# RWKV layer of a hybrid trunk: r as three fp32r products, weights split one layer earlier, inputs and joins moved

## Chip, cores and metric

One core of a Trainium2 chip runs the whole program once. The metric is device time in microseconds. TensorE is called PE, its weight loads PEld, VectorE DVE, ScalarE ACT, GpSimd POOL and SyncE SP, as in the profile.

## What is computed

Two layers on 256 tokens of width 1024. Each layer is FFN, mixer, FFN and a gated per-layer embedding, with RMS norms around every part. The mixer of layer 0 is a gMLP, that of layer 1 an RWKV-7 time mixer. The change touches the RWKV mixer and the FFN in front of it:

```python
dx = shift(h) - h
x_rkv = h[:, :, None, :] + dx[:, :, None, :] * mu[:3]
r, k, v = einsum('bsnd,nde->bsne', x_rkv, w_in)          # three 1024 x 1024 products
zw = w0 + tanh((h + dx * mu[3]) @ w1) @ w2               # decay
a  = sigmoid(a0 + ((h + dx * mu[4]) @ a1) @ a2)
g  = sigmoid((h + dx * mu[5]) @ g1) @ g2                 # gate
kk = normalised(k * k_k); k = k * (1 + (a - 1) * k_a)
S_t = S_{t-1} diag(w_t) + (S_{t-1} a_t) b_t^T + v_t k_t^T;  y_t = S_t r_t
out = ((group_norm(y) + bonus) * g) @ w_out
swiglu(x) = (silu(gate) * up) @ w2,  gate, up = split(x @ w13)   # the FFN
```

All inputs are float32, D = 1024, 16 heads of 64, D_FF = 2816.

## The kernel before

**Weights.** `self.units` is the list of all weight pieces, in the order in which the program wants them. Most are 128 x 1024 pieces in three steps. `emit_dma` (L127) loads one into one of four `raw` buffers. `emit_split` (L137) takes one of 20 slots of 128 x 2048 and writes the fp32r high half (ACT, L154) and the remainder (DVE, L156) into it. A product is then three fp32r products: high by high, low by high, high by low (`mm3`, L178 to L180). A piece with a fourth entry is not split: it is loaded as it is, 1 MB at a time, into a slot (L146), and multiplied as float32, which the profile shows as two records for each product. `pump(k, reserve)` emits up to k pieces if slots are left, `need(i)` emits all pieces up to i at once, `release(i)` gives the slot back. Slots and the eight PSUM banks are handed out first in, first out, so each user waits for the last user of the same slot or bank.

**Order on the engines.** The program is written in one order; the framework places the instructions of each engine in a queue, where a later instruction can go ahead of an earlier one that is not ready, and adds the waits. `with behind(name)` keeps the instructions of its block behind a named one of the same engine.

**The FFN ahead of RWKV.** Eleven column blocks c. From c = 2 on, one iteration is `AT(c)` (L400, 64 products: 32 of 512 columns and 32 of 256) and the down products of block c - 2 (`Dn`, L178 to L180, 24 of 512 columns). Each iteration uses six pieces: four of w13 and two of w2.

**RWKV** (`rwkv`, one function with inner helpers), in program order:
- `K(0)`, `K(1)`: k, 16 steps of three fp32r products; then `l1()`, the first product of decay and a.
- `xprod(n)` (L819, DVE): the input h + dx mu of one of the six uses, eight pieces of 128 x 256. `xprod(0)` for r comes here; `xprod(5)` for the gate and `xprod(2)` for v come after the decay.
- `low(g)`: second product of decay and a, with ACT's tanh and sigmoid. `squares(i)` (ACT), `knorm(b)` (L895 to L904: DVE, ACT, POOL) and `ktr(b)` (PE transposes, L913).
- For each half i: `decay(i)` (L999 to L1004, DVE), `ab(i)` (L1010 to L1013), some of r's eight steps (`r_step`, L1055, float32, 256 columns) and `triangle(i)` (L1039, small products, copied out by ACT).
- The substitution (L1091, L1093, DVE, 15 steps that depend on each other), two transposes (L1094, L1095).
- rT copies (L1250), `xprod(5)`, `gate1` (L1171), `xprod(2)`, the products that form kT, sk and rT x gam (L1256 to L1269).
- v: eight steps of eight records (`v_step`, L1307, float32, 512 columns). Between them the gate's second product, and four `join`s, which put the 16 x 16 inverses together (small products: L1110, L1121, L1136, L1150). `join(0)` to `join(2)` stand among steps 5 to 7. `inside(k)` (L1284 to L1294) forms one of eight pairs of masked products: PE, DVE, PE. `inside(0)` to `(3)` stand among the v steps, `(4)` and `(5)` behind them.
- `tb` transposes, `join(3)`, `inside(6)`, `inside(7)`, then the mean of v and `stack_v` (L1389, DVE, eight pieces).
- Four `chunk`s, each depending on the one before: `us` (L1415, L1441), `y`, `st` (L1453), with L1443, L1444 and L1458 on ACT and DVE between. Between the chunks stand weight splits and `vgain` (L1244, L1245). Then the output product (`Dn`, `o`).

Of the kernel before, what the change touches and what calls it, by code (L numbers as in the profile page):

```python
# [60 lines left out]
class Trunk:  # L61
    NSLOT = 20

    def __init__(self, ctx, tc, io):
        self.tc = tc
        self.nc = tc.nc
        self.io = io
        self.uid = 0
        ep = lambda name, bufs=1, **k: ctx.enter_context(tc.tile_pool(name=name, bufs=bufs, **k))
        self.slots = ep("slots")  # L70
        self.pp = ep("pp", space=bass.MemoryType.PSUM)
        self.rawp = ep("raw", 4)
# [17 lines left out]
        self.pq = {}  # L90

# [35 lines left out]
    def emit_dma(self):  # L127
        i = self.n_dma
        self.n_dma += 1
        if len(self.units[i]) > 3:  # L130
            return
        src, p, n = self.units[i]
        t = self.rawp.tile([128, 1024], F32, name="raw", tag="raw")
        self.nc.sync.dma_start(t[:p, :n], src)
        self.raw[i] = t

    def emit_split(self):  # L137
# [3 lines left out]
        if len(self.units[i]) > 3:  # L141
# [8 lines left out]
        src, p, n = self.units[i]  # L150
# [155 lines left out]
    def ffn_units(self, f):  # L306
# [468 lines left out]
    def rwkv_units(self):  # L775
# [9 lines left out]
        put("r", rows(0))  # L785
# [6 lines left out]
    def rwkv(self, at):  # L792
# [20 lines left out]
        def xprod(n, lo=0, hi=T, ks=range(KT)):  # L813
# [135 lines left out]
        xprod(0)  # L949
        wu_ = self.slot("wu")  # L950
# [100 lines left out]
        def r_step(k):  # L1051

            w = self.need(at["r"] + k // 2)[0][:, k % 2]
            for m in range(KT):
                mm(psr[m // 2][:, (m % 2) * T:(m % 2 + 1) * T], lhsT=w[:, m * 128:(m + 1) * 128], rhs=xent(0, k),  # L1055
                   start=k == 0 and m % 2 == 0, stop=k == KT - 1 and m % 2 == 1)
            if k % 2:
                self.release(at["r"] + k // 2)
# [12 lines left out]
        self.drop(eo)  # L1071
        self.drop(X["x"][0])
# [22 lines left out]
        V.transpose(xt.rearrange("p n t -> p t n"), Wu)  # L1095
# [173 lines left out]
        V.tensor_tensor(kT, kT, rT, op=ALU.mult)  # L1269
        self.drop(gam, ta, rT)  # L1270
# [54 lines left out]
        v_step(3)  # L1325
        v_step(4)
# [13 lines left out]
        v_step(7, join(2))  # L1340
# [6 lines left out]
        inside(4)  # L1347
        inside(5)
# [27 lines left out]

        sv = [self.slot("sv") for _ in range(2)]
        svv = [t.rearrange("p (c m h t) -> p c m h t", c=2, m=8, h=2) for t in sv]
        vv = vn.rearrange("p (b m h t) -> p b m h t", b=2, m=8, h=2)
        vm = self.small(32, "vm", 1)  # L1380
        vmv = vm.rearrange("p (b m h) -> p b m h", b=2, h=2)
        for b in range(NB):
            V.tensor_reduce(vm[:, b * 16:(b + 1) * 16], vn[:, b * D:(b + 1) * D].rearrange("p (h t) -> p h t", t=64), axis=AX.X, op=ALU.add)
            V.tensor_scalar(vm[:, b * 16:(b + 1) * 16], vm[:, b * 16:(b + 1) * 16], ck[:, 0:1], 1.0 / 64, op0=ALU.mult, op1=ALU.mult)

        def stack_v(c):
            rs = half[c % 2]
            for h in range(2):
                V.scalar_tensor_tensor(svv[c // 2][half[1 - h], c % 2, :, h, :], vv[rs, c // 2, :, h, :], ck[rs, 0:1],  # L1389
                                       vmv[rs, c // 2, :, h].unsqueeze(2).to_broadcast([64, 8, 64]), op0=ALU.mult, op1=ALU.subtract)  # L1390

        for c in range(NCH):
            stack_v(c)
        G.memset(svv[0][EV, 0, :, 0, :], 0.0)
        G.memset(svv[0][OD, 0, :, 1, :], 0.0)
# [284 lines left out]
```

## Time and profile before

| | us |
|---|---|
| median of 3 runs | 1177.98 |
| lowest, highest | 1177.35, 1180.4 |
| the profiled execution | 1183.38 |
| its span, first to last instruction | 1181.6 |

The profile is that of one execution. Times in it are counted from the start of its span. The RWKV stage lies between about 745 us (first product of k) and 958 us, the FFN ahead of it between about 565 and 745. An engine's queue is in order: an instruction that waits holds up all behind it. The idle time ahead of an instruction is put down to what ended last by semaphore events.

### The profile page before, as it was taken

Reading aid. Unit: us, or ns where it says so; the run is one execution under the profiler, and the core shown is the slowest. Engines: PE = TensorE matmul, PEld = TensorE weight load, DVE = VectorE, ACT = ScalarE, POOL = GpSimd, SP = SyncE. Lnnn points to the kernel's source line nnn. Section 1 sums busy time; section 2 is a strip of 40 time slices with the busy share of each in tenths; the row PEclk is TensorE's granted clock in tenths of the full one; section 3 lists DMA queues with packets and bytes.
Section 4 is the critical chain, followed back from the end, with each engine's and each line's share of the span. In section 5 each row is a group of like instructions: output and inputs, shape, how many; then the busy total and the mean of one; then the engine's idle time right before and its main releaser. Section 6 shows DMA issues by size and latency. Waiting matters only on the chain. (4 is left out here: it accounts for less than half of the span.)

```text
span 1181.6 us, 18709 instructions
## 1 busy us (share of the span) xinstructions
PE 1151.2 (97%) x7284; PEld 954.3 (81%) x7284; DVE 859.1 (73%) x1299; ACT 659.7 (56%) x1145; POOL 72.5 (6%) x92
## 2 busy tenths in 40 slices
PE   8999999999999999999999999999998899999997
PEld 6788888888888888888888888777467778888886
DVE  5886666877678666667876666878859898676663
ACT  6665556545476555558755554374226396555553
POOL 0000000010010000001100000230000220000011
PEclk8999999999999999999999999999989999999999
DMA  7886654746586666646766664550300377666510
GB/s 244 292 295 196 190 172 152 253 156 205 186 271 202 194 192 184 192 134 196 248 189 194 193 192 144 178 183 1 125 4 21 108 249 263 193 189 193 177 47 36
DMA packets 58841, 207.78 MB, mean 176 GB/s; under 512 B 6784, under 2 KB 7296, under 8 KB 58496
## 3 DMA queue, kind: packets, MB, share of 16 engines
q1 hardware_dynamic: 58752, 206.59, 54.8%
q8 instruction: 57, 0.93, 0.3%
q14 instruction: 32, 0.26, 0.1%
HBM read 205.51 MB, written 1.05 MB: 175 GB/s over the span
## 5 line engine op out<-in xcount | busy, mean ns | idle before, releaser
L156 DVE TENSOR_TENSOR w<-raw,w 128x1024 fp32r<-128x1024 f32 x348 | 423.6, 1223 | 145.6 <-ACT w L154 139.8
L154 ACT CAST w<-raw 128x1024 fp32r<-128x1024 f32 x348 | 366.3, 1055 | 153.9 <-PE mm L400 68.7
L400 PE MATMUL mm<-xT,w 128*128 128x512 f32 (+1 forms) x2304 | 407.8, 337 | 0.0
L400 PEld LDWEIGHTS mm<-xT,w 128*128 128x128 f32 x2304 | 358.6, 189 | 50.0
L178 PE MATMUL acc<-w,hT 128*128 128x512 f32 x352 | 138.2, 393 | 0.0
L179 PE MATMUL acc<-w,hT 128*128 128x512 f32 x352 | 137.3, 390 | 0.0
L180 PE MATMUL acc<-w,hT 128*128 128x512 f32 x352 | 137.1, 389 | 0.0
L408 ACT COPY pn<-mm 128x256 f32<-128x256 f32 x144 | 46.6, 375 | 93.8 <-PE mm L400 93.8
L409 DVE TENSOR_TENSOR pn<-mm,pn 128x256 f32<-128x256 f32 x144 | 54.4, 418 | 39.3 <-ACT pn L408 39.3
L180 PEld LDWEIGHTS acc<-w,hT 128*128 128x128 f32 x352 | 66.1, 188 | 14.1
L178 PEld LDWEIGHTS acc<-w,hT 128*128 128x128 f32 x352 | 66.2, 188 | 12.6
L179 PEld LDWEIGHTS acc<-w,hT 128*128 128x128 f32 x352 | 66.3, 188 | 12.3
L232 POOL TENSOR_SCALAR rpost<-ss 128x1 f32<-128x1 f32 x15 | 7.5, 500 | 777.9 <-ACT junk L239 777.9
L178 PE MATMUL mm<-w,xT 128*128 128x512 f32 x128 | 51.8, 415 | 2.9 <-ACT w L154 2.6
L289 DVE SCALAR_TENSOR_TENSOR xT<-tr,gT,xT 128x128 fp32r<-128x128 f32 x112 | 35.6, 344 | 24.4 <-ACT xT L288 23.5
L179 PE MATMUL mm<-w,xT 128*128 128x512 f32 x128 | 51.4, 405 | 0.7 <-DVE xT L289 0.5
L412 DVE TENSOR_TENSOR pn<-pn,yc 128x512 f32<-128x512 f32 x72 | 49.7, 691 | 2.0
L180 PE MATMUL mm<-w,xT 128*128 128x512 f32 x128 | 50.9, 403 | 0.0
L179 PE MATMUL z<-w,xT 128*128 128x512 f32 x128 | 49.9, 390 | 0.0
L180 PE MATMUL z<-w,xT 128*128 128x512 f32 x128 | 49.9, 390 | 0.0
L178 PE MATMUL z<-w,xT 128*128 128x512 f32 x128 | 49.7, 393 | 0.0
L288 ACT ACTIVATE xT<-tr,gT 128x128 fp32r<-128x128 f32 x112 | 37.8, 371 | 19.3 <-PE tr L275 14.9
(282 smaller groups left out, 1534.8 us busy)
## 6 DMA issues: line engine op xcount, KB each, us to landing
raw<-in_w SPq DMA_DIRECT2D x264, 512.0 KB, 4.3
raw<-in_win SPq DMA_DIRECT2D x32, 512.0 KB, 4.4
raw<-in_wout SPq DMA_DIRECT2D x16, 512.0 KB, 4.8
raw<-in_wg SPq DMA_DIRECT2D x16, 512.0 KB, 3.9
wf<-in_wrkv SPq DMA_DIRECT2D x8, 1024.0 KB, 5.1
gbc<-in_norm_g SPq DMA_DIRECT2D x9, 512.0 KB, 5.4
raw<-in_wrkv SPq DMA_DIRECT2D x8, 512.0 KB, 3.5
raw<-in_bwout SPq DMA_DIRECT2D x8, 512.0 KB, 3.6
```

The lines of the kernel that those rows point to most:

```text
L154: self.high = self.nc.scalar.copy(hh, r[:p, :n])
L156: eng.tensor_tensor(ll, r[:p, :n], hh.bitcast(F32), op=ALU.subtract)
L178: mm(out, lhsT=lh, rhs=rh, start=start, stop=False)
L179: mm(out, lhsT=ll, rhs=rh, start=False, stop=False)
L180: mm(out, lhsT=lh, rhs=rl, start=False, stop=stop)
L232: nc.gpsimd.tensor_scalar(r, a, b, eps, op0=ALU.add, op1=ALU.add)
L288: done = (nc.scalar.activation(hi, v, AF.Copy, scale=gc), nc.vector.scalar_tensor_tensor(lo, v, gc, hi.bitcast(F32), op0=ALU.mult, op1=ALU ...
L289: nc.vector.scalar_tensor_tensor(lo, v, gc, hi.bitcast(F32), op0=ALU.mult, op1=ALU.subtract))
L400: nc.tensor.matmul(ps[i][:, :T] if s else ps[i], lhsT=w[:, sl], rhs=x, start=u + q + s == 0, stop=s + u == 2 and q == 3)
L408: nc.scalar.copy(zi, ps[i][:, T:])
L409: nc.vector.tensor_tensor(zi, ps[i][:, :T], zi, op=ALU.add)
L412: nc.vector.tensor_tensor(z2, z2, rbc.unsqueeze(1).to_broadcast([128, 2, T]), op=ALU.mult)
```

## The change

- **Weights of r.** Eight new pieces stand among the units of the FFN ahead, one behind each of eight iterations' w2. They are loaded and split like the others; then the 1 MB slot with both halves is stored to DRAM (`flush`, at the next split) and given back. In RWKV r's units become eight loads of 1 MB of these pairs, where they were four loads of 1 MB with two pieces each.
- **r.** `parts` splits r's input (two ACT copies, two DVE subtractions of 128 x 1024), and `r_step` makes three fp32r products of 256 columns where it made one float32 product. Each step gives its slot back and pumps one piece.
- **Inputs.** `xprod(5)` and `xprod(2)` move from behind the decay to right behind `xprod(0)` and `parts`.
- **kT x rT** (L1269) moves behind the second transpose of the substitution.
- **Joins.** `join(0)` to `join(2)` stand among v steps 3 to 5, `inside(4)` and `inside(5)` inside v steps 6 and 7. One weight piece fewer is pumped ahead of the joins.
- **Stack of v.** The mean and `stack_v` of the first half move ahead of the `tb` transposes; the rest goes behind chunk(0) and chunk(1).

```diff
     def emit_split(self):
...
+        self.flush()
+        if len(self.units[i]) > 4:
+            t = self.slot("w", F32R)
+            self.nc.sync.dma_start(t.bitcast(F32), self.parts.pop(self.units[i][3]))
+            self.hl[i] = (t, t[:, :1024], t[:, 1024:])
+            self.n_split += 1
+            return
...
+        if len(self.units[i]) > 3:
+            self.stores.append((self.units[i][3], hl))
+        else:
+            self.hl[i] = (hl, hh, ll)
...
+    def flush(self):
+        for key, hl in self.stores:
+            t = self.parts[key] = self.rdp.tile([128, 2048], F32, name=f"part_{key}", tag=f"part_{key}")
+            self.nc.sync.dma_start(t, hl.bitcast(F32))
+            self.drop(hl)
+        self.stores.clear()
...
         for c in range(2, FC):
             put(at13, c, w13(c))
             put(at2, c - 2, w2(c - 2))
+            for _ in range(-(-len(early) // (FC - c))):
+                key, src = early.popleft()
+                u.append((src, 128, 1024, key))
...
-        put("r", rows(0))
+        put("r", [(None, 128, D, f"r{k}", True) for k in range(KT)])
...
+        def parts(n, key, engs):
+            X[key] = [self.slot("xs", F32R) for _ in range(2)]
+            for i, e in enumerate(engs):
+                ks = slice(i * KT // len(engs), (i + 1) * KT // len(engs))
+                x, xh, xl = (g8(t)[:, ks] for t in (X["x"][n], *X[key]))
+                S.copy(xh, x)
+                L[key] = e.tensor_tensor(xl, x, xh.bitcast(F32), op=ALU.subtract)
+            self.drop(X["x"].pop(n))
...
         xprod(0)
+        parts(0, "r", (V, V))
+        P(1, 8)
+        xprod(5)
+        xprod(2)
+        self.drop(hnT, dxT)
...
         def r_step(k):
-            w = self.need(at["r"] + k // 2)[0][:, k % 2]
+            wh, wl = self.need(at["r"] + k)
+            xh, xl = (g8(t)[:, k] for t in X["r"])
             for m in range(KT):
-                mm(psr[m // 2][:, (m % 2) * T:(m % 2 + 1) * T], lhsT=w[:, m * 128:(m + 1) * 128], rhs=xent(0, k),
-                   start=k == 0 and m % 2 == 0, stop=k == KT - 1 and m % 2 == 1)
+                o, ms = psr[m // 2][:, (m % 2) * T:(m % 2 + 1) * T], slice(m * 128, (m + 1) * 128)
+                mm(o, lhsT=wh[:, ms], rhs=xh, start=k == 0 and m % 2 == 0, stop=False)
+                mm(o, lhsT=wh[:, ms], rhs=xl, start=False, stop=False)
+                mm(o, lhsT=wl[:, ms], rhs=xh, start=False, stop=k == KT - 1 and m % 2 == 1)
+            self.release(at["r"] + k)
+            if k < 7:
                 P(1, 1)
...
-        xprod(5)
         gate1()
-        xprod(2)
-        self.drop(hnT, dxT)
...
-        v_step(3)
-        v_step(4)
...
-        v_step(5, join(0))
+        v_step(3, join(0))
+        with behind("sub"):
+            V.tensor_tensor(kT, kT, rT, op=ALU.mult)
+        self.drop(rT)
         inside(0)
         inside(1)
-        v_step(6, join(1))
+        v_step(4, join(1))
...
         inside(2)
         inside(3)
-        v_step(7, join(2))
+        v_step(5, join(2))
+        v_step(6, [lambda: None, lambda: inside(4)])
+        v_step(7, [lambda: None, lambda: inside(5)])
...
-        inside(4)
-        inside(5)
+        mean_v(0)
+        stack_v(0)
+        G.memset(svv[0][EV, 0, :, 0, :], 0.0)
+        G.memset(svv[0][OD, 0, :, 1, :], 0.0)
+        stack_v(1)
...
         chunk(0)
         with behind("c"):
+            mean_v(1)
+            stack_v(2)
             P(1, 0)
             vgain(0)
         chunk(1)
         with behind("c"):
+            stack_v(3)
             P(1, 0)
             vgain(1)
```

`mean_v(b)` and `stack_v(c)` are the old reduction, scaling and stacking of v, as functions; `L["sub"]` is the second transpose of the substitution.

## Rows read from the trace of the kernel before

**Rows 1.** The page, part 1: busy time, share, instructions.
```profile
PE 1151.2 (97%) x7284; PEld 954.3 (81%) x7284; DVE 859.1 (73%) x1299; ACT 659.7 (56%) x1145; POOL 72.5 (6%) x92
```

**Rows 2.** Stretches: length, busy time of each engine (instructions), clock, DMA share, GB/s.
```profile
60.00:90.00 30.00, 30.00 (x160) 25.85 (x159) 24.85 (x37) 19.62 (x31) 1.07 (x1) 1.00 0.88 289
660.00:680.00 20.00, 20.00 (x109) 17.27 (x108) 14.37 (x22) 10.63 (x19) 0.00 (x0) 1.00 0.64 196
...
860.00:880.00 20.00, 19.78 (x418) 11.30 (x419) 9.96 (x13) 3.72 (x6) 0.00 (x0) 0.75 0.01 2
880.00:900.00 20.00, 16.52 (x391) 13.71 (x390) 17.74 (x31) 13.64 (x31) 1.05 (x2) 1.00 0.01 2
```

**Rows 3.** PE's waits, 740 to 960: total, times, longest.
```profile
PE us L1415 <- DVE sv L1389: 2.7, 1, 2.7
PE g L1171 <- ACT rT L1250: 2.4, 1, 2.4
PE rb L1292 <- issue: 2.0, 1, 2.0
```

**Rows 4.** Groups by line and shape, 770 to 980: count, busy, mean of one.
```profile
L1055 PE MATMUL r<-xr,wf 128*128 128x256 f32 x128 | 28.4, 381 | 0.1
...
L819 DVE SCALAR_TENSOR_TENSOR xr<-dxT,chT,hnT 128x256 f32<-128x256 f32 x20 | 9.3, 475 | 0.0
...
L1269 DVE TENSOR_TENSOR kT<-kT,rT 128x2048 f32<-128x2048 f32 x1 | 2.3, 2281 | 0.0
```

**Rows 5.** Groups by line and shape, PE, 600 to 740.
```profile
L400 PE MATMUL mm<-xT,w 128*128 128x512 f32 x256 | 63.9, 391 | 0.0
L400 PE MATMUL mm<-xT,w 128*128 128x256 f32 x256 | 35.7, 282 | 0.0
```

**Rows 6.** Timeline of DVE, 762 to 786: start, length, instruction, count [idle before].
```profile
769.97 1.66 DVE L819 SCALAR_TENSOR_TENSOR xr<-dxT,chT,hnT 128x256 f32<-128x256 f32 x4
772.01 1.29 DVE L895 TENSOR_TENSOR kn<-k,gbc 128x512 f32<-128x512 f32 x2 [0.39 <-PE k L180]
...
782.29 1.22 DVE L999 SCALAR_TENSOR_TENSOR eo<-eo,q 128x1024 f32<-128x1024 f32 x1 [6.44 <-ACT eo L994]
```

**Rows 7.** Groups by line, 600 to 740: the two halves of a split.
```profile
L156 DVE TENSOR_TENSOR w<-raw,w 128x1024 fp32r<-128x1024 f32 x47 | 57.5, 1222 | 26.0 <-ACT w L154 25.1
...
L154 ACT CAST w<-raw 128x1024 fp32r<-128x1024 f32 x47 | 49.7, 1056 | 22.8 <-PE mm L400 18.0 <-PE acc L180 4.9
```

**Rows 8.** Timeline of all engines, from the last transposes of k to the joins.
```profile
783.82 1.63 PE L913 MATMUL tr<-ident,kn 128*128 128x128 f32 x12 [0.83 <-ACT kk L914]
785.54 14.08 PE L1055 MATMUL r<-xr,wf 128*128 128x256 f32 x64
...
819.15 0.16 DVE L1091 TENSOR_TENSOR pn<-wu 128x2 f32<-128x2 f32 x1
819.63 0.48 DVE L819 SCALAR_TENSOR_TENSOR xr<-dxT,chT,hnT 128x256 f32<-128x256 f32 x1
820.22 4.58 PE L1171 MATMUL g<-wf,xr 128*128 128x160 f32 x32 [2.37 <-ACT rT L1250]
...
841.22 7.99 PE L1307 MATMUL v<-wf,xr 128*128 128x512 f32 x18
...
843.97 2.12 DVE L1094 STREAM_TRANSPOSE wu<-wu 128x1024 f32<-128x1024 f32 x1
```

**Rows 9.** Timeline, 894 to 960: DVE's stack of v, first product of chunk(0).
```profile
897.44 6.14 DVE L1389 SCALAR_TENSOR_TENSOR sv<-vn,ck,vm 64x512 f32<-64x512 f32 x8
...
898.33 0.42 PE L1415 MATMUL us<-sv,sk 128*64 128x64 f32 x4 [2.70 <-DVE sv L1389]
```

**Rows 10.** Timeline of the FFN ahead: one AT, and the raw loads of k.
```profile
697.72 21.81 SPq L134 DMA_DIRECT2D raw<-in_wrkv  x8
...
700.00 11.31 PE L400 MATMUL mm<-xT,w 128*128 128x512 f32 x64
```

**Rows 11.** The page, part 6: size, median time from issue to landing.
```profile
wf<-in_wrkv SPq DMA_DIRECT2D x8, 1024.0 KB, 5.1
```

More of the change, by code (lines that the diff above doesn't have):

```diff
@@ L90, in __init__ @@
         self.pq = {}
+        self.parts = {}
+        self.stores = []
     def slot(self, name, dt=F32):
@@ L129, in emit_dma @@
         self.n_dma += 1
-        if len(self.units[i]) > 3:
+        if len(self.units[i]) > 4:
             return
-        src, p, n = self.units[i]
+        if len(self.units[i]) > 3 and not isinstance(self.units[i][3], str):
+            return
+        src, p, n = self.units[i][:3]
         t = self.rawp.tile([128, 1024], F32, name="raw", tag="raw")
@@ L140, in emit_split @@
             self.emit_dma()
-        if len(self.units[i]) > 3:
+        self.flush()
+        if len(self.units[i]) > 4:
+            t = self.slot("w", F32R)
+            self.nc.sync.dma_start(t.bitcast(F32), self.parts.pop(self.units[i][3]))
+            self.hl[i] = (t, t[:, :1024], t[:, 1024:])
+            self.n_split += 1
+            return
+        if len(self.units[i]) > 3 and not isinstance(self.units[i][3], str):
             src, p, n, k = self.units[i]
@@ L149, in emit_split @@
             return
-        src, p, n = self.units[i]
+        src, p, n = self.units[i][:3]
         hl = self.slot("w", F32R)
@@ L156, in emit_split @@
         eng.tensor_tensor(ll, r[:p, :n], hh.bitcast(F32), op=ALU.subtract)
-        self.hl[i] = (hl, hh, ll)
+        if len(self.units[i]) > 3:
+            self.stores.append((self.units[i][3], hl))
+        else:
+            self.hl[i] = (hl, hh, ll)
         self.n_split += 1
@@ L303, in xpairs, with ffn_units @@
         return t, [[Halves(*(q[:, :, s, b * 128:(b + 1) * 128] for q in v)) for s in range(2)] for b in range(NB)]
-    def ffn_units(self, f):
+    def ffn_units(self, f, early=()):
         io = self.io
@@ L315, in put @@
             u.extend(l)
+        early = deque(early)
         put(at13, 0, w13(0))
@@ L1070, in rwkv @@
         r_step(7)
-        self.drop(eo)
-        self.drop(X["x"][0])
+        self.drop(eo, *X["r"])
         P(1, 3)
@@ L1094, in rwkv @@
         V.transpose(wv.rearrange("p n s -> p s n"), Wu.rearrange("p t s -> p s t"))
-        V.transpose(xt.rearrange("p n t -> p t n"), Wu)
+        L["sub"] = V.transpose(xt.rearrange("p n t -> p t n"), Wu)
         def pieces(n, do, last):
@@ L1268, in rwkv @@
                 V.tensor_tensor(skv[g][half[h], :, h, :, 64:128], gs(rT, g)[half[h]], gs(gam, g)[half[h]], op=ALU.mult)
-        V.tensor_tensor(kT, kT, rT, op=ALU.mult)
-        self.drop(gam, ta, rT)
+        self.drop(gam, ta)
         rb_ = self.slot("rb")
@@ L1346, in rwkv, with mean_v, stack_v @@
         self.unbank(*psv[0], *psv[1])
-        inside(4)
-        inside(5)
+        sv = [self.slot("sv") for _ in range(2)]
+        svv = [t.rearrange("p (c m h t) -> p c m h t", c=2, m=8, h=2) for t in sv]
+        vv = vn.rearrange("p (b m h t) -> p b m h t", b=2, m=8, h=2)
+        vm = self.small(32, "vm", 1)
+        vmv = vm.rearrange("p (b m h) -> p b m h", b=2, h=2)
+        def mean_v(b):
+            V.tensor_reduce(vm[:, b * 16:(b + 1) * 16], vn[:, b * D:(b + 1) * D].rearrange("p (h t) -> p h t", t=64), axis=AX.X, op=ALU.add)
+            V.tensor_scalar(vm[:, b * 16:(b + 1) * 16], vm[:, b * 16:(b + 1) * 16], ck[:, 0:1], 1.0 / 64, op0=ALU.mult, op1=ALU.mult)
+        def stack_v(c):
+            rs = half[c % 2]
+            for h in range(2):
+                V.scalar_tensor_tensor(svv[c // 2][half[1 - h], c % 2, :, h, :], vv[rs, c // 2, :, h, :], ck[rs, 0:1],
+                                       vmv[rs, c // 2, :, h].unsqueeze(2).to_broadcast([64, 8, 64]), op0=ALU.mult, op1=ALU.subtract)
+        mean_v(0)
[3 more added lines that the diff above has]
+        stack_v(1)
         bn = [self.slot("bn") for _ in range(2)]
@@ L1375, in rwkv @@
         self.drop(bt, kt)
[L1377 to L1395, printed above, removed]
         yo = self.slot("yo")
@@ L1572, in run @@
             if st[0] == "ffn":
-                plan.append(self.ffn_units(st[1] * 2 + st[2]))
+                early = []
+                if names[i + 1:i + 2] == ["rwkv"]:
+                    early = [(f"r{k}", self.io["wrkv"][0, k * 128:(k + 1) * 128, :]) for k in range(KT)]
+                plan.append(self.ffn_units(st[1] * 2 + st[2], early))
             elif st[0] == "ple":
```

2 lines of the change are left out of this document (removed).

## Prediction

> **What bounds the kernel now.** I read the page's busy times first, then the stretches, then PE's waits, then the timeline of the RWKV stage. PE is busy for 97% of the span [rows 1]; in the FFN ahead of RWKV it has no gap at all (20.00 of 20.00 us at 660 to 680 [rows 2]). So time is won only where PE does less, or where it stands still, and it stands still only in the RWKV stage: 2.7 us ahead of `us`, 2.4 us ahead of the gate's first product, 2.0 us inside `inside()` [rows 3]. The stretch 860 to 880 also shows a mean granted clock of 0.75 [rows 2]: the lower of TensorE's two levels (1.2 GHz instead of 2.4) for half of it, 10 us, which as PE is busy then costs about 5 us. Two other readings matter. DVE is nearly full at 880 to 900 (17.74 of 20) and half idle at 860 to 880 (9.96) [rows 2]. And in the FFN the transfers move some 196 GB/s, while at 60 to 90 they move 289 GB/s with PE at 30.00 of 30.00 [rows 2].
>
> **r in three products.** Today r costs PE 28.4 us: 64 products of 256 columns, two records each [rows 4]. Afterwards it is 8 x 8 x 3 = 192 products of fp32r with 256 columns. The FFN's L400 has this very shape: 256 of them fill 35.7 us, in 32 runs of eight, so a run takes 1.116 us, and less the last one's 0.282 us the seven before it take 0.119 us each [rows 5]. With every product at that pace r takes 22.8 us, plus 0.7 us for the ends of four stretches: 23.5, a gain of 4.9. If a run's end were paid for every eight, it is 192 x 0.1395 = 26.8, a gain of 1.6. I take 4.9, since the 24 products of one step follow each other without a change of form.
>
> The Trainium skill (FP8 and Floating Point Precision, TensorE Precision Notes) says that true FP32 takes four passes through the array. By that, three products cost three quarters, 21.3 us, and the gain would be 7.1, 2.2 more than by the rows. The rows show less, and the measured pace decides.
>
> **Inputs ahead of the decay.** The change puts two DVE subtractions (128x1024, 1.22 each by L156 [rows 7]) and 16 of `xprod`'s pieces (four take 1.66 us, so 0.40 each back to back [rows 6]) ahead of the decay: 2.4 + 6.4 = 8.8 us. DVE was free there from 771.63 (the end of `xprod(0)`) to L999 at 782.29, 10.66 us, less some 2.8 us of `knorm(1)`'s own (L895 1.29 and smaller ones): 7.8 us of cover [rows 6]. So the decay starts 1.0 us late at least, 8.8 at most. I take 1.6, because the two reductions of `knorm(1)` now fall behind the new work and beside the decay. The two ACT copies (1.06 us each [rows 7]) go beside `xprod(0)`; without that cover they add 2.1 us.
>
> What waits for it: `knorm(1)` stands behind the new work in the program, so L895 moves from 772.01 to about 780.4. `low(2)` uses the two banks that `knorm(1)` empties, and r's first bank is one that `low(2)` empties. I put r's start at 787.0 instead of 785.54 [rows 8] (between no delay and the full 8.4), and the last transposes of `ktr(1)` (1.63 us [rows 8]) now fall inside r. So r's side loses 1.5 + 1.6 us of the 4.9.
>
> **The gate.** The 2.4 us ahead of L1171 [rows 3] are put down to ACT's rT copies, but the product starts at 820.22, right behind the first piece of `xprod(5)` (819.63 to 820.11 [rows 8]), which DVE does only after the decay. With `xprod(5)` done early this wait goes: 2.4 us. v then starts 4.9 + 2.4 - 1.5 - 1.6 = 4.2 us earlier, at 820.4 for 824.6.
>
> **Joins.** The substitution (L1091, L1093) runs from 819.15 to L1094 at 843.97 [rows 8], 24.8 us of DVE. Out of it go 16 pieces of 0.475 (7.6), kT x rT (2.28) [rows 4] and one weight split (1.22 [rows 7]): 13.7, or 15.1 with the overlaps of neighbours taken out (about 0.08 for each of 18, as four pieces of 0.475 take 1.66 [rows 4, 6]). It starts 1.8 us later (triangle(1) now follows DVE, not PE), so L1094, of about 2.1 us, ends at 838.1 for 846.1. PE begins v's step ahead of the joins at 841.22 - 4.2 [rows 8], and its first piece of join(0) one product of 0.9 us later, at 837.9. Both meet within half a microsecond, and any further delay of DVE is paid by PE one for one. From join(0) on the work is the same, with two v steps more (6.9 us) that came before join(0) until now: these joins gain nothing by themselves. What they do gain is that `inside(4)` and `inside(5)` lie beside v, so that DVE forms `stack_v(0)` before chunk(0). The wait of 2.7 us ahead of `us` [rows 3, 9] goes; as DVE is nearly full at 880 to 900 I leave 1.0 of it: a gain of 1.7.
>
> **Chunks.** `mean_v(1)`, `stack_v(2)` and `stack_v(3)` (four of L1389's eight pieces, 3.1 of its 6.14 us [rows 9], and a reduction of the size of a split's subtraction, some 1.3) move behind chunk(0) and chunk(1). Before, DVE worked off its stack until 903.6, 5.3 us into chunk(0), which began at 898.33 [rows 9]; now it idles there and gets 4.4 us later on, where it has no room. Bounds: 0 (the splits of `o` give way) and 4.4 lost. I take 1.7.
>
> **The FFN ahead.** Eight more splits: 8 x 1.22 of DVE and 8 x 1.06 of ACT [rows 7] in a stretch where DVE is busy 14.37 and ACT 10.63 of 20 us [rows 2], about 0.6 us more in each iteration of 16.8 us (L400's 11.31 [rows 10], and 24 products of 512 columns, 0.229 each by the same reading of L400's 512-column runs [rows 5]: 1.997 a run, less 0.391, over seven). They are hidden: the splits run far ahead, k's raw loads are issued from 697.72 [rows 10], 48 us before k's first product. Uncovered they would cost 9.8 us. The transfers grow from six to seven units of 0.524 MB plus a store of 1.05 MB: 4.72 MB in 16.8 us, 281 GB/s, just under the 289 that a stretch holds with a full PE [rows 2]. No row shows a large store beside loads; if its bytes cost as much as read ones, nothing is lost; at twice that it is (3.67 + 2.10) / 16.8 = 343 GB/s, 19% over 289, or some 25 us in 134. I take nothing, the nearest row being loads of the same size. The SP queue gets eight stores, each queued behind its split, and the raw loads behind the store wait for that same split's buffer anyway. In RWKV four more loads of 1 MB go between 784 and 803, each into a buffer that l, kn or an earlier r step leaves; at r's pace of 2.9 us a step and 5.1 us a load [rows 11] they arrive ahead of the step by 6 us or more.
>
> **Sum.** -4.2 - 1.7 + 1.7 = -4.2 us. The profiled execution took 1183.4 (span 1181.6), 5.4 over the median of 1177.98; I move the difference as it stands: 1173.8.
>
> **Rivals.**
> (B) The low clock goes. It came after a stretch of small products with a 2.0 us stop in `inside()` [rows 3]. The same pieces come again in the same order, which speaks for a dip of the same length; but they start elsewhere in time, and the longer stop ahead of `us` met no dip (1.00 at 880 to 900 [rows 2]). Without the dip 5 us more are gained: 1168.8. The Trainium skill (TensorE: Matmul & The Clock Gate, Part 1) says that activity releases the throttle and idling brings it back; by that rule this case, with one stop fewer, would be the likelier one. The rows do not decide it.
> (C) DVE eats the gain: if the decay is late by 5 to 8.8 us instead of 1.6, join(0) waits for L1094 by 3 to 7 us, at the price of one for one: 1177 to 1181. For it: the meeting point has half a microsecond of slack. Against it: 7.8 us of idle cover.
> (D) Slower: the FFN runs short of transfers. Its place is the eight iterations that carry a store. It decides where a stored byte costs over 1.15 read ones (1.15 x 1.05 + 3.67 = 4.87 MB in 16.8 us is 289 GB/s); at 1.5 the need is 312 GB/s, 8% over, 10 us in 134: 1183.8. Against it: loads run 48 us ahead, which swallows part of that.
> That the change does not do what it says (r at the old price) would be L400's pace failing; the row is of the same shape, so I give it no chance of its own: it would give 1178.7 and lies in C.
>
> **How the numbers follow.** Forecast 0.40 (its own range 1171 to 1177, two thirds of it more than 0.3% faster), B 0.23, C 0.20, D 0.17. What a measurement here can tell from no change is 0.3%, 3.5 us. Faster: 0.27 + 0.23 = 0.50. Same: 0.13 + 0.14 of C = 0.27. Slower: 0.17 + 0.06 of C = 0.23. The range takes in B below and D's likeliest price above: 1166 to 1184.
>
> **What would show it.** In the profile after: 192 records of r at about 0.12 us from start to start; r's first product near 787, `ktr(1)`'s transposes inside it; no wait ahead of the gate; L1094 ending near 838 and join(0) right behind; under 1 us ahead of `us`; PE at 20.00 of 20 through the FFN, with 280 GB/s. Wrong would make it: a PE gap ahead of join(0) or triangle(0), idle PE in the FFN, a clock dip of another length, or chunk(1) and chunk(2) longer by more than 2 us together.

## The result, and the profile after

The changed kernel takes 1185.87 us (median of 6 runs, 1184.64 to 1188.24) beside 1177.97 of the kernel before on the same chip (6 runs): a ratio of 1.0061, 95% interval 1.0049 to 1.0073. It is slower by 0.6%, some 7 us; the forecast was 1173.8, and 1184 was the end of the range. The profiled execution of after took 1188.24 us, its span is 1186.4. The profiled execution of before lies 5.4 us above its median, that of after 2.4, so their spans differ by 4.8 us and the medians by 7.9.

The page's busy times answer [rows 1]: PE does 1.3 us less, DVE 11 us more.

```profile
PE 1149.9 (97%) x7348; PEld 957.8 (81%) x7348; DVE 870.4 (73%) x1309; ACT 666.3 (56%) x1155; POOL 76.5 (6%) x92
```

So the loss is no added work of TensorE: it waits somewhere, or runs at the lower clock. In the FFN ahead it does neither. The stretches after answer [rows 2] (length, PE, PEld, DVE, ACT, POOL, clock, DMA share, GB/s):

```profile
640.00:660.00 20.00, 20.00 (x111) 17.39 (x111) 14.43 (x21) 11.79 (x19) 0.00 (x0) 1.00 0.84 296
660.00:680.00 20.00, 20.00 (x105) 17.12 (x104) 13.44 (x19) 9.59 (x16) 0.00 (x0) 1.00 0.80 284
...
860.00:880.00 20.00, 19.77 (x394) 11.85 (x394) 11.68 (x15) 3.80 (x6) 1.05 (x2) 1.00 0.01 2
```

PE has no gap at 284 to 296 GB/s (before: 184 to 196 in the same stretches), and k's first product starts at 745.42 after, 745.83 before. The dip of the clock at 860 to 880 (0.75 in [rows 2]) is gone. From the first output product to the end of the span it is 251.7 us after, 251.2 before. So the whole difference of the two traces lies between k's first product and the output's: 189.3 us after, 184.6 before.

**Place one: `knorm(1)`.** DVE's timeline after answers [rows 6] (start, length, instruction, count [idle before]):

```profile
773.82 7.66 DVE L846 SCALAR_TENSOR_TENSOR xr<-dxT,chT,hnT 128x256 f32<-128x256 f32 x15
781.40 1.27 DVE L932 TENSOR_TENSOR kn<-k,gbc 128x512 f32<-128x512 f32 x2
782.60 1.21 DVE L1041 SCALAR_TENSOR_TENSOR eo<-eo,q 128x1024 f32<-128x1024 f32 x1
...
788.32 0.16 DVE L938 TENSOR_SCALAR gn<-gn 128x16 f32<-128x16 f32 x1
...
797.34 2.36 DVE L1110 TENSOR_TENSOR bt<-kk,a 128x1024 f32<-128x1024 f32 x2 [3.52 <-ACT kk L951]
```

Of the 16 pieces of `xprod(5)` and `xprod(2)`, 15 run as one block, and `knorm(1)`'s first product (L895 before, L932 after) starts 9.4 us later, at 781.40 for 772.01. The decay (L999, now L1041) starts on time, 782.60 for 782.29, and cuts in between `knorm(1)`'s parts, so L938 comes at 788.32. Behind it stand two steps of POOL. Before, and then after:

```profile
775.93 2.90 POOL L902 TENSOR_TENSOR gn<-gn,mhalf 128x16 f32<-128x16 f32 x1 [0.74 <-DVE gn L901]
778.91 1.90 POOL L904 TENSOR_TENSOR kn<-kn,gn 128x1024 f32<-128x1024 f32 x1
```

```profile
788.56 2.90 POOL L939 TENSOR_TENSOR gn<-gn,mhalf 128x16 f32<-128x16 f32 x1 [12.02 <-DVE wu L1027]
791.54 3.97 POOL L941 TENSOR_TENSOR kn<-kn,gn 128x1024 f32<-128x1024 f32 x1
```

`knorm(1)` is done at 795.5 instead of 780.8, and PE waits for it (timeline of PE after, answering [rows 8]):

```profile
784.55 1.75 PE L1009 MATMUL l<-pn,wf 64*128 64x256 f32 x8 [1.94 <-ACT kn L936]
787.02 1.97 PE L950 MATMUL tr<-ident,kn 128*128 128x128 f32 x8 [0.72 <-ACT kT L951]
788.64 0.56 PE L1099 MATMUL r<-xs,w 128*128 128x256 f32 x1
...
795.57 1.97 PE L950 MATMUL tr<-ident,kn 128*128 128x128 f32 x8 [4.24 <-POOL kn L941]
```

After the stop of 1.94 us the granted clock falls to TensorE's lower level (1.2 GHz) and stays there over the stop of 4.24 us: in stretches of 5 us it is 0.59, 0.50 and 0.54 from 785 to 800.

```profile
785.00:790.00 5.00, 4.28 (x22) 3.69 (x21) 4.88 (x8) 5.00 (x13) 1.44 (x1) 0.59 0.57 196
790.00:795.00 5.00, 1.34 (x7) 1.04 (x5) 3.67 (x5) 0.39 (x2) 4.92 (x2) 0.50 0.10 39
795.00:800.00 5.00, 4.43 (x23) 4.43 (x24) 2.66 (x3) 3.01 (x6) 0.52 (x1) 0.54 0.25 66
```

The second triangle follows at 819.43, 7.3 us later than before (812.12), and v starts 4.1 us later, although r's products are shorter and the gate no longer waits:

```profile
823.82 0.28 PE L1100 MATMUL r<-xs,w 128*128 128x256 f32 x1
823.94 0.28 PE L1101 MATMUL r<-xs,w 128*128 128x256 f32 x1
824.06 0.28 PE L1099 MATMUL r<-xs,w 128*128 128x256 f32 x1
...
824.42 4.51 PE L1215 MATMUL g<-wf,xr 128*128 128x160 f32 x32
828.77 1.02 PE L1347 MATMUL v<-wf,xr 128*128 128x512 f32 x2
```

**Place two: the chunks.** The first product over `us` starts at 895.03, 3.3 us earlier than before [rows 9]. The stretch from v to it is 7.4 us shorter, but not all of that is won by the joins: the dip at 860 to 880, up to 5 us, and the wait of 2.7 us ahead of `us` lay in it before. From there to the first output product it is 39.6 us for 32.1. PE's waits in this stretch (total, times, longest) answer [rows 3]:

```profile
PE st L1496 <- DVE sv L1487: 2.7, 1, 2.7
PE us L1484 <- ACT k L1460: 2.1, 1, 2.1
PE us L1458 <- ACT bn L1424: 0.9, 1, 0.9
```

and the clock falls twice, at 900 to 910 and at 920 to 930:

```profile
900.00:905.00 5.00, 4.58 (x74) 3.90 (x76) 1.86 (x5) 1.32 (x4) 0.00 (x0) 0.70 0.01 3
905.00:910.00 5.00, 5.00 (x102) 4.63 (x100) 4.89 (x8) 2.11 (x6) 0.00 (x0) 0.62 0.19 50
...
920.00:925.00 5.00, 2.32 (x33) 1.89 (x31) 4.94 (x10) 3.44 (x5) 1.46 (x2) 0.74 0.28 105
925.00:930.00 5.00, 5.00 (x95) 4.77 (x93) 4.76 (x11) 2.09 (x5) 0.52 (x1) 0.57 0.34 110
```

DVE waits at the very place from which the stack work was taken, 5.01 us ahead of the copy of `us`, and is full later, when PE waits 2.7 us for the same copy (L1487):

```profile
895.86 0.75 DVE L1424 COPY bn<-tb 64x256 f32<-64x256 f32 x2
901.62 0.77 DVE L1487 COPY sv<-us 64x256 f32<-64x256 f32 x2 [5.01 <-ACT sv L1486]
```

The earlier wait, 2.1 us for L1460, is not DVE's: ACT does that copy only behind a weight split and six copies of `bn`.

```profile
896.59 1.05 ACT L166 CAST w<-raw 128x1024 fp32r<-128x1024 f32 x1
897.66 2.26 ACT L1424 COPY bn<-tb 64x256 f32<-64x256 f32 x6
899.95 0.65 ACT L1460 COPY k<-us 128x256 f32<-128x256 f32 x2
```

### The profile page after: what moved, and what is told of

Same layout as the page of the kernel before. It is cut to its first block, busy times and chain, and to the rows that moved or that the text cites. A ratio compares the mean times of both kernels' runs of the same rounds, so it can differ in the third digit from the quotient of the medians.

```text
span 1186.4 us, 18900 instructions
## 1 busy us (share of the span) xinstructions
PE 1149.9 (97%) x7348; PEld 957.8 (81%) x7348; DVE 870.4 (73%) x1309; ACT 666.3 (56%) x1155; POOL 76.5 (6%) x92
## 4 chain that ended last, share of the span: by engine, by line
PE 71%; DVE 13%; DMA 7%; ACT 4%; issue 3%; POOL 2%; SPq 0%; POOLq 0%; DVEq 0%; ACTq 0%
PE mm L427 27%; PE acc L201 6%; PE acc L202 6%; PE acc L203 6%; DMA raw<-in_w 6%; DVE w L168 4%; PE z L202 2%; PE z L201 2%; PE z L203 2%; PE v L1347 2%; ACT w L166 2%; PE mm L202 2%; PE mm L203 2%; PE mm L201 2%; DVE xr L846 2%
## 5 line engine op out<-in xcount | busy, mean ns | idle before, releaser
L168 DVE TENSOR_TENSOR w<-raw,w 128x1024 fp32r<-128x1024 f32 x356 | 433.1, 1223 | 151.1 <-ACT w L166 146.6
L166 ACT CAST w<-raw 128x1024 fp32r<-128x1024 f32 x356 | 373.3, 1054 | 168.7 <-DMA raw<-in_w 71.5
L202 PEld LDWEIGHTS acc<-w,hT 128*128 128x128 f32 x352 | 66.3, 188 | 12.6 <-DVE hT L444 0.3
L440 ACT ACTIVATE k<-pn 128x256 f32<-128x256 f32 x72 | 30.1, 418 | 37.9 <-DVE pn L439 37.8
```

What stands on the lines that cost most here:

```text
L166: self.high = self.nc.scalar.copy(hh, r[:p, :n])
L168: eng.tensor_tensor(ll, r[:p, :n], hh.bitcast(F32), op=ALU.subtract)
L202: mm(out, lhsT=ll, rhs=rh, start=False, stop=False)
L440: nc.scalar.activation(sg, z[:, :T], AF.Silu)
```

## The experiments

Theory Q: the input pieces stand ahead of `knorm(1)` in DVE's queue, and what hangs on it (POOL, transposes, triangles) is late. Theory S: stack work put between the chunks goes where DVE has no room. Rival F: the FFN, with splits, stores and eight loads. Later theories came up: P (POOL's product is held up by DVE's work, e8), D (from r's start on the decay's chain on DVE sets the second triangle and v, e11) and J (the joins need a substitution free of v's pieces, e12). Each kernel ran beside the kernel before; "share" is its time against that. All kernels in one table, from their profiled executions, in us from k's first product: r, the second triangle, v, `us`, the first output product o. "Low" is the length of low clock between 745 and 940, summed over stretches of 5 us as (1 - clock) x 10; at most half of it is lost, less where PE waits anyhow.

| kernel | time | share, 95% interval | r | triangle 2 | v | us | o | low |
|---|---|---|---|---|---|---|---|---|
| before | 1177.97 | 1 | 39.7 | 66.3 | 78.8 | 152.5 | 184.6 | 13.6 |
| after | 1185.87 | 1.0061 (1.0049 to 1.0073) | 43.2 | 74.0 | 83.4 | 149.6 | 189.3 | 27.4 |
| e1 | 1179.38 | 1.0010 (0.9996 to 1.0023) | 45.0 | 68.2 | 77.5 | 142.4 | 181.8 | 17.0 |
| e2 | 1179.56 | 1.0009 (0.9993 to 1.0025) | 43.2 | 74.4 | 83.8 | 148.4 | 181.5 | 13.7 |
| e3 | 1175.40 | 0.9964 (0.9952 to 0.9977) | 44.4 | 68.2 | 77.5 | 142.7 | 175.9 | 3.4 |
| e4 | 1190.99 | 1.0102 (1.0075 to 1.0129) | 55.0 | 81.7 | 91.6 | 160.8 | 193.3 | 17.0 |
| e5 | 1179.01 | 1.0009 (0.9998 to 1.0019) | 39.7 | 66.3 | 80.5 | 149.3 | 181.9 | 6.8 |
| e6 | 1184.44 | 1.0051 (1.0035 to 1.0068) | 39.7 | 66.3 | 80.4 | 150.3 | 189.4 | 20.4 |
| e7 | 1177.46 | 0.9990 (0.9978 to 1.0001) | 44.3 | 68.2 | 77.5 | 145.9 | 178.1 | 6.9 |
| e8 | 1180.88 | 1.0025 (1.0014 to 1.0037) | 46.7 | 74.1 | 84.6 | 149.8 | 183.2 | 13.6 |
| e9 | 1181.80 | 1.0021 (1.0006 to 1.0036) | 40.9 | 67.2 | 77.8 | 149.3 | 182.6 | 20.5 |
| e10 | 1175.50 | 0.9974 (0.9963 to 0.9986) | 41.9 | 68.8 | 79.5 | 143.9 | 179.0 | 6.8 |
| e11 | 1176.82 | 0.9981 (0.9968 to 0.9993) | 39.7 | 66.4 | 76.4 | 145.0 | 178.4 | 10.3 |
| e12 | 1176.41 | 0.9971 (0.9959 to 0.9984) | 41.0 | 67.6 | 74.1 | 143.0 | 177.9 | 6.8 |

One execution differs from the next by several us, mostly in "low", so places are read from this table and times from the shares.

The mean granted clock of the whole span is on record for every execution, and gives the length of low clock in the same way. On average it is 32.0 us in after (6 executions), 24.3 in e1, 22.7 in e2, 15.0 in e3 (10 each), 28.0 in e6 (6), 15.2 in e5 (11) and 15.6 in the kernel before (94). The profiled execution of before has 26 us.

**e1, inputs behind `knorm(1)`.**

```diff
         P(1, 8)
-        xprod(5)
-        xprod(2)
-        self.drop(hnT, dxT)
...
         knorm(1, p1)
+        xprod(5)
+        xprod(2)
+        self.drop(hnT, dxT)
```

> The changed kernel with one edit: xprod(5) and xprod(2) stand behind knorm(1) in the program, still ahead of the decay. Theory Q (DVE's queue: the 16 pieces ahead of knorm(1) make its first product late by 9.4 us, PE stops and drops to the lower clock): L932 of the second half back at 772 to 774 instead of 781.4, no low-clock stretch at 786 to 800, v's first product near 820 instead of 828.8, time about 1178 instead of 1185.9. Theory S (the loss is made in the chunks alone): time stays within 2 us of 1185.9, v's start moves but chunk(0) does not gain. Theory F (weights split in the FFN and r's loads cost it): no change, 1185 to 1187.

The share falls from 1.0061 to 1.0010, 0.51% or 6.0 us. The second triangle comes 5.8 us earlier against k, v 5.9, and `knorm(1)`'s first product stands at 769.81. Q holds, though not in every sign: PE's wait for L941 stays at 4.2 us, r starts 1.8 us later, and 6.8 us of low clock are left at 780 to 790. What is won is the time of the last transposes, which PE starts 41.6 us behind k's first product instead of 50.2; DVE no longer waits ahead of `bt`.

**e2, stack work back.** All of it stands behind the second half's `inside` again, nothing behind chunk(0) and chunk(1).

```diff
-        mean_v(0)
-        stack_v(0)
...
-        stack_v(1)
...
         self.drop(bt, kt)
+        for b in range(NB):
+            mean_v(b)
+        for c in range(NCH):
+            stack_v(c)
...
-            mean_v(1)
-            stack_v(2)
...
-            stack_v(3)
```

> The changed kernel with the whole stack of v (both means, four stack_v) back behind the tb transposes, ahead of chunk(0). Theory S (the 4.4 us of DVE moved between the chunks delay the chunk chain): first us product to first o product 32 to 34 us instead of 39.7, the wait ahead of us back at 2 to 3 us, in all 3 to 5 us faster, about 1182. Theory Q alone: chunk stage no shorter than 38, time 1185 to 1188 (the us wait comes back).

1.0009: 0.52%, 6.1 us, more than the 3 to 5 us that S gave. From `us` to o it takes 33.1 us for 39.6, no clock dip lies in it. ACT's copy of `us` comes ahead of the last six copies of `bn`, at 895.39, and PE waits 0.9 us for it instead of 2.1. The stack work runs in DVE's 5 us gap again, beside PE's first chunk:

```profile
895.53 4.58 DVE L1404 SCALAR_TENSOR_TENSOR sv<-vn,ck,vm 64x512 f32<-64x512 f32 x6
900.14 0.77 DVE L1488 COPY sv<-us 64x256 f32<-64x256 f32 x2
```

**e3, both together.**

> Both edits of the two runs before in one kernel. If Q and S both hold, their gains add: about 1174, 0.3% faster than before. If only Q holds: 1178 to 1180. If neither: 1185 to 1188.

0.9964: faster than before by 0.36%, the best of the study. The two effects add up (0.51 + 0.52 against 0.97 measured). Low clock is 3.4 us for 27.4. So Q and S together are more than the loss against before (0.61%). Part of it is the low clock that comes with the stops: by the average lengths above (7.7 and 9.3 us less than in after, half of it lost at most) about 3.9 of e1's 6.0 us and 4.7 of e2's 6.1 at the most. The other 2.1 and 1.4 us at least are the stops themselves. The averages are of 6 to 10 executions, so these bounds are rough.

**e4, the inputs moved in the kernel before, alone.**

```diff
         xprod(0)
+        xprod(5)
+        xprod(2)
+        self.drop(hnT, dxT)
...
-        xprod(5)
         gate1()
-        xprod(2)
-        self.drop(hnT, dxT)
```

> The kernel before with one part of the change: xprod(5) and xprod(2) right behind xprod(0), r as it was (float32, unsplit), joins and stack as they were. Theory Q: knorm(1) is late here too, r starts 3 to 9 us later than 785.5, and the 2.4 us ahead of the gate are gone: 1180 to 1186, slower than before. Theory F (r's part is to blame, the inputs are harmless): 2 us faster than before, about 1176.

1.0102, 12 us: the move alone is slower than the whole change, and by more than Q had given (1180 to 1186). PE waits 10.0 us for L904 in two stops, r starts at 55.0.

```profile
768.86 6.44 POOL L904 TENSOR_TENSOR kn<-kn,gn 128x1024 f32<-128x1024 f32 x1
783.57 2.90 POOL L902 TENSOR_TENSOR gn<-gn,mhalf 128x16 f32<-128x16 f32 x1 [8.28 <-DVE gn L901]
786.55 2.47 POOL L904 TENSOR_TENSOR kn<-kn,gn 128x1024 f32<-128x1024 f32 x1
```

Here a new thing shows: the same product on POOL takes 1.90 us before, 6.44 and 2.47 here.

**e5, splits and stores alone.** The kernel before, with r's pieces split and stored in the FFN, but r in float32 from the old loads.

```diff
+                if names[i + 1:i + 2] == ["rwkv"]:
+                    early = [(f"r{k}", self.io["wrkv"][0, k * 128:(k + 1) * 128, :]) for k in range(KT)]
```

> The kernel before with one part of the change alone: r's eight weight pieces are read, split on ScalarE and VectorE and stored to DRAM during the layer's FFN ahead, and nobody reads them back; r stays in full fp32. Theory Q plus S (the loss lies in the queue of VectorE ahead of knorm(1) and in the stack work between the chunks, the FFN hides its part): k's first product where it is in the kernel before (745.8 us in its trace, within 1 us), time 1177 to 1180 us. Rival F (the splits and stores take the FFN's weights late, the rival D of the prediction): TensorE waits appear in the FFN, k's first product 5 to 10 us later, time 1183 to 1189 us.

1.0009 (0.9998 to 1.0019), k's first product at 744.53 (745.83 before), so it is not late. F is refuted for splits and stores, up to the 0.19% of the interval. The eight loads are not in this run; in after no wait of PE for a load shows.

**e6, joins and stack work in the kernel before.** The change's hunks on joins, kT x rT and stack, nothing else.

> The kernel before with the joins among v's fourth to sixth step and with the pieces that moved behind the first two chunks (means and stacks of v), without the splits, with r in full fp32 and with the inputs of gate and v where the kernel before has them. Theory S: v's first product where it was (824.6 us); the first product over us some 7 us earlier than 898.3, as the stretch from the substitution to the last join shrank by 7 us in the changed kernel; then 6 to 7 us more between it and the first output product than the 32.1 us of the kernel before; time within 3 us of before, 1176 to 1181 us. Rival (the joins bring nothing, as the prediction had it, and only the stack work costs): 1183 to 1186 us.

1.0051, 1184.44 us: the rival's time, not that of S, though S's 6 to 7 us between `us` and o came: it takes 39.0 us (32.1 before), with the same waits as after (L1483, the L1487 of after, 2.7; L1456, its L1460, 2.1). The stack work costs in the kernel before what it costs in the changed one; low clock can be much of that, with 12.8 us more of it on average than in e5. v to `us` takes 69.9 us beside 68.8 in e5: the 7 us I had expected from the joins did not come. A stop of 1.9 us without a cause in the profile and 6.8 us of low clock behind it lie in this stretch (843 to 855), so a gain of 2 or 3 us could be hidden in it.

**e7, r and inputs without joins and stack work.** e3 with joins as before.

> The changed kernel with r in three products and its splits, with the inputs of gate and v right behind knorm(1), and with the joins and the stack work back where the kernel before has them. Against the kernel with inputs behind knorm(1) and stack work back alone (1175.4 us), this tells what the joins bring. If the joins bring the 7 us that the stretch from the substitution to the last join lost in the changed kernel: v's first product at 822 to 823 us, first product over us near 896 us, time 1180 to 1183 us. If joins bring nothing by themselves (the prediction): 1174 to 1177 us.

0.9990. Against e3 (0.9964) the joins are worth 0.26%, 3 us by the shares and 2.1 by the medians, up to 1.8 of them low clock (18.6 us on average in e7); the time is just above the range where joins bring nothing (1174 to 1177), well below the 1180 to 1183 of the other theory. `us` waits 2.7 us for the stack here as in [rows 3], and not for the stack in e3.

**e8, `knorm`'s last product on DVE.** Theory P: POOL is held up by DVE. In e3 (POOL, DVE and PE's wait):

```profile
780.98 5.94 POOL L941 TENSOR_TENSOR kn<-kn,gn 128x1024 f32<-128x1024 f32 x1
```

```profile
777.67 5.23 DVE L846 SCALAR_TENSOR_TENSOR xr<-dxT,chT,hnT 128x256 f32<-128x256 f32 x13
782.81 1.21 DVE L1038 SCALAR_TENSOR_TENSOR eo<-eo,q 128x1024 f32<-128x1024 f32 x1
783.95 1.22 DVE L1039 SCALAR_TENSOR_TENSOR eo<-eo,tw 128x1024 f32<-128x1024 f32 x1
785.20 2.80 DVE L1040 SCALAR_TENSOR_TENSOR q<-eo 128x1024 f32<-128x1024 f32 x1
```

```profile
PE tr L950 <- POOL kn L941: 5.0, 2, 4.2
```

```diff
-            G.tensor_tensor(k3, k3, s.unsqueeze(2).to_broadcast([128, 16, 64]), op=ALU.mult)
+            V.tensor_tensor(k3, k3, s.unsqueeze(2).to_broadcast([128, 16, 64]), op=ALU.mult)
```

> The kernel with inputs behind knorm(1) and stack work back (1175.4 us), with knorm's last product, 128x1024, on VectorE in place of GpSimd. There it took 5.94 us on GpSimd while VectorE ran the input pieces, against 1.90 us in the kernel before where VectorE stood idle, and TensorE waited 4.24 us for it. Theory P (GpSimd is held up by VectorE's work beside it): the product takes near 1.2 us on VectorE, the wait of TensorE ahead of ktr(1) falls under 1.5 us, r's first product 2.5 to 4 us earlier than 789.7 us, time 1171.5 to 1173.5 us. Rival (VectorE's queue is what is short, so another 1.2 us there, twice, costs as much as it gives): 1175 to 1177 us.

Missed by both: 1.0025. The product takes 1.22 us on DVE, as expected, and PE's waits for it are gone. But DVE now waits for the power on POOL (L939, some 3 us) at the head of its queue, with everything behind it:

```profile
772.79 1.22 DVE L941 TENSOR_TENSOR kn<-kn,gn 128x1024 f32<-128x1024 f32 x1 [2.88 <-POOL gn L939]
...
785.24 1.22 DVE L941 TENSOR_TENSOR kn<-kn,gn 128x1024 f32<-128x1024 f32 x1 [2.80 <-POOL gn L939]
```

The decay starts at 790.34 (782.81 in e3): the two waits and the two products, 8.1 us, account for it. The wait has moved from PE to DVE, where it costs more.

**e9, inputs back at the old place.** e3 with `xprod(5)` ahead of `gate1()` and `xprod(2)` behind it.

> The changed kernel with the stack work back and with the inputs of gate and v back where the kernel before has them, right ahead of and behind the gate's products; r in three products and the joins stay. In the kernel with the inputs behind knorm(1) (1175.4 us) TensorE waits 4.2 us for knorm's last product, which takes 5.94 us on GpSimd beside VectorE's input pieces. Theory P (that product is slow because VectorE works beside it): here VectorE stands idle again then, the product takes 1.9 us, the wait is under 1 us, r's first product lies 40 to 42 us behind k's first (44.4 there, 39.7 before), the 2.4 us wait of the gate for its inputs comes back, v's first product 75 to 76.5 us behind k's (77.5 there): 1173 to 1175 us, so the inputs ahead of the decay give nothing at all. Rival (moving the inputs ahead is what brought the gain): v's first product 79 us or more behind k's, 1177 to 1180 us.

L941 takes 1.90 us again and r starts at 40.9: P holds there. But v starts at 77.8 (77.5 in e3), and the time, 1.0021, is worse than either theory's. Three waits of PE say why:

```profile
PE m L1078 <- DVE wu L1122: 2.5, 1, 2.5
...
PE m L1078 <- DVE bt L1049: 1.0, 1, 1.0
...
PE q L1151 <- DVE wu L1135: 1.3, 1, 1.3
```

r comes 3.5 us earlier and waits ahead of the triangles for DVE's decay. And v's eight pieces stand between those of the substitution, so that `join(0)` waits 1.3 us. Behind that wait the clock falls:

```profile
840.00:845.00 5.00, 3.66 (x72) 1.47 (x68) 4.93 (x5) 1.07 (x2) 0.00 (x0) 0.86 0.63 210
845.00:850.00 5.00, 5.00 (x132) 2.69 (x132) 4.06 (x3) 0.00 (x0) 0.00 (x0) 0.50 0.02 3
850.00:855.00 5.00, 5.00 (x101) 3.46 (x101) 2.67 (x3) 0.58 (x1) 0.00 (x0) 0.50 0.36 108
```

**e10, the product on DVE with the gate's pieces in between.** e3, for the second half only.

```diff
+            if between:
+                between()
-            G.tensor_tensor(k3, ...)
+            (V if between else G).tensor_tensor(k3, ...)
...
-        knorm(1, p1)
-        xprod(5)
+        knorm(1, p1, lambda: xprod(5))
```

> The kernel with inputs behind knorm(1) and stack work back (1175.4 us), with the last product of knorm(1) alone on VectorE, and between it and the power on GpSimd, for which it waits, the eight input pieces of the gate; v's eight pieces follow it. In the earlier try VectorE stood 2.9 and 2.8 us for the power with nothing in between. Theory P with Q (what costs is the order on VectorE, no lack of its time): no stand of VectorE at that product, TensorE's wait ahead of ktr(1) under 1 us, r's first product 40 to 41 us behind k's first (44.4 there), v's 73.5 to 75 us behind (77.5 there), 1171.5 to 1173.5 us. Rival (from r's start on the decay's chain on VectorE sets v's start, so r comes early and waits inside): r's first product early, more waits of r's stretch for VectorE, v's 77 us behind k's, 1174.5 to 1176 us.

0.9974, 1175.50: the rival's time, though v starts at 79.5 us where it had 77. DVE still waits 1.21 us ahead of the product, r starts 2.5 us earlier than in e3, and the second triangle then waits 2.2 us for DVE (L1126) and the first 1.9.

**e11, e3 without the split of r.** r in float32 from the old loads, no splits and stores, no `parts`.

> The kernel with inputs behind knorm(1) and stack work back (1175.4 us), with r in full fp32 again and without the splits and stores of its weights; the inputs behind knorm(1) and the joins among v's fourth to sixth step stay. If r's shorter products bring what the prediction counted (4.9 us): v's first product 82 us or more behind k's first (77.5 there, 78.8 in the kernel before), 1179 to 1181 us. Theory D (from r's start on the decay's chain on VectorE sets the second triangle and with it v's start, whatever r takes): the two pieces that make r's low parts are gone from VectorE as well, v's first product 78 to 80 us behind k's, 1176 to 1178 us.

0.9981, 1176.82, the time that theory D had. v starts at 76.4 us, earlier than D's 78 to 80 and than in e3 (77.5) with its shorter r: r starts 4.7 us earlier here (39.7 for 44.4), as POOL's product starts 1.0 us sooner without `parts` and takes 2.88 us for 5.94; PE waits 1.0 us for it, not 4.2. DVE has a gap of 0.75 us between the pieces and the decay here, and none in e3.

```profile
780.66 2.88 POOL L941 TENSOR_TENSOR kn<-kn,gn 128x1024 f32<-128x1024 f32 x1
782.53 2.09 DVE L1036 SCALAR_TENSOR_TENSOR eo<-eo,q 128x1024 f32<-128x1024 f32 x1 [0.75 <-ACT eo L1031]
```

The intervals of the two shares overlap (0.9968 to 0.9993, 0.9952 to 0.9977): what the three products bring beside the rest is 0.17% at the middle and can't be told from nothing.

**e12, v's inputs behind `knorm(1)`, the gate's at the old place.** On e3.

> The kernel with the stack work back, v's eight input pieces right behind knorm(1), the gate's eight pieces where the kernel before has them, ahead of the gate's products. With both sets at the old place (1181.8 us) v's pieces stood between those of the substitution, the first join waited 1.3 us and a stretch of low clock followed; with both behind knorm(1) it was 1175.4 us. Theory J (the joins at their new place need a substitution free of v's pieces, and the gate's pieces cost nothing in VectorE's idle stretch ahead of the gate): no wait of the first join, v's first product 77 to 78.5 us behind k's, 1174 to 1176 us. Rival (any piece left behind the decay costs): 1178 to 1181 us.

0.9971, 0.4 us above what I had given J (1174 to 1176), and well under e9. `join(0)` does not wait for DVE and the clock stays up at 840 to 860 (1.00). v's first two products slip in ahead of the gate's, at 74.1, so that figure is none of v's start. J holds: the joins at their new place need the substitution free of v's pieces.

## Why the prediction was wrong

**Right.** r's pace: 0.12 us from start to start at full clock, as [rows 5] said. (By the four passes that the Trainium skill, FP8 and Floating Point Precision, TensorE Precision Notes, gives true FP32, an estimate is 21.3 / 192 = 0.11; the trace is slower.) The gate's 2.4 us went. The splits and stores in the FFN cost 0.19% at most, by e5. The 2.7 us ahead of `us` fell to 0.9, and the joins with it are worth 2 to 3 us (e7 against e3), near the 1.7 of the sum.

**The step that failed first: what hangs on `knorm(1)`.** The prediction put L895 at 780.4 (781.40 measured) and saw that r's side loses, but took 1.5 + 1.6 us for it. It followed `knorm(1)` on DVE and PE and left out its two steps on POOL, 2.90 and 3.97 us, the decay cutting in ahead of its reductions, and the 3.52 us for which DVE then waits ahead of `bt`. The decay, for which it took 1.6 us, was on time (0.3 us late). It also took 7.8 us of DVE's "idle cover" for free. Of that time POOL needed 1.90 us with DVE quiet, and the work of `knorm(1)` lay in the middle of it. Measured by e1: 6.0 us, up to 3.9 of them low clock.

**The term that was mis-sized: the chunks.** 1.7 us lost was forecast, bounds 0 to 4.4; e2 measured 6.1, and e6 shows the same stretch longer in the kernel before. The 4.4 us of DVE were hidden before, in the gap that DVE has while PE works at the first half of chunk(0); the prediction saw that DVE would idle there and get the work where it has no room, so the mechanism was right and the size was not. Their new place delays a copy of `us` on DVE (2.7 us). The wait of 2.1 us for ACT's copy was not in the sum. Low clock can be up to 4.7 of the 6.1 us; without it the term might have stayed within its bounds, which no run here shows.

**The gain that went nowhere: r.** The sum let v start earlier by all of r's 4.9 us. Two things take them. In e3 r starts 4.7 us later than in e11, which differs in r alone: `parts` (2.4 us of DVE) stands among the steps of `knorm(1)`, and POOL's product is done 4.1 us later. And from r's start on the second triangle has two conditions, r's steps in front of it and the decay's chain on DVE. With r in float32 both are met at 66.3 to 66.4 us (before, e5, e6, e11, no wait of PE). With three products r's steps are done sooner and PE waits: 0.6 us in e3, and where r starts early in spite of `parts`, 2.2 (e10) and 2.5 (e9, e12); the triangle is at 67.2 to 68.8. DVE was level with PE there, and `parts` and the inputs even lengthen its chain. No rival had that.

**The rivals.** C ("DVE eats the gain") named the engine, but at another place (L1094 against `join(0)`; DVE's two transposes were in time after) and at 1177 to 1181. B asked whether the low clock would go. It went where B looked (860 to 880), but fell at 785 to 800 and 900 to 910 instead and longer at 920 to 930: 27.4 us of it against 13.6. The forecast had kept the total as it was. B's 5 us were not there to be had in full: the sum goes from the median of before, but the dip is one of a profiled execution with 26 us of low clock and 5.4 us over that median, where others have 15.6 on average. It followed a stop of 2.0 us put down to `issue`, that is, to nothing that the profile shows; stops of the same kind, of 1.9 and 1.8 us, stood ahead of low clock at 845 to 855 in e6 and e11. What made the clock fall is only told by what stood ahead: stops of PE of 1.94 and 4.24 us, 2.14 and 2.68 us after, 1.34 us in e9. Stops of that size do not always bring it (2.7 us ahead of `us` before). How the loss of e1 and e2 divides between stops and clock is known only within the bounds above.

With both moves undone (e3) the time is 0.36%, 4.2 us, below before: the forecast's sum, but by luck, with other terms in it (joins 2 to 3, and r's products, if anything, 2).

## What to carry to other kernels

Ahead of a moved step, don't count an engine's idle time but ask which instruction of another engine it was idle for: here DVE's gaps were the time in which POOL finished `knorm(1)` and PE the first half of chunk(0). Work that is put into such a gap must stand behind, in program order, whatever the other engine waits for. And before a shorter product is credited, look at the next product that depends on another engine: if that engine arrives now without slack, the gain ends there.

## What the runs showed of the hardware

POOL's product (128x1024) takes 1.90 us with DVE quiet and 2.2 to 6.4 beside it. In e3 it spans 780.98 to 786.92; DVE's pieces run on at full pace, 0.40 us each, until one (L1040 at 785.20) takes 2.80 us instead of 1.23 and ends 1.1 us behind POOL's. That is how it would look if POOL waited until about 785.0, then ran its 1.9 us, and DVE waited meanwhile. In e11 the pieces end at 781.78, the product 1.8 us later, and the DVE step that starts in between (782.53) takes 2.09 us for 1.2. In after it takes 3.97 us beside one long DVE step that starts with it (L1029, 2.29 us), about the sum of 1.90 and that step. e9 shows the other order: POOL starts first (782.44, 1.90 us), and DVE's first step of the decay (783.86) takes 1.56 us for 1.22. The Trainium skill (SBUF — State Buffer, Who interferes with whom) says that a DVE instruction with two SBUF inputs contends with a GpSimd instruction that reads SBUF, and that the one that issues second blocks until the first is through. The traces agree with the blocking. In e3, read in this way, POOL waited through several DVE instructions, not through one.

A store of 1 MB took 8.1 us from issue to landing (median of 8), a load of the same size 4.8 to 5.1, and 284 to 296 GB/s of both together left PE without a gap.
